# Last stage of a two-layer trunk: raw gate weights in two places and on GpSimd's queue, output weights kept as split parts, and the first split ordered into the stage before

## Chip, cores and metric

The kernel runs on one core of a Trainium2 chip. The metric is the device time of one execution in microseconds. The engines are PE (TensorE), DVE (VectorE), ACT (ScalarE), POOL (GpSimd) and SP (SyncE, which here only issues transfers). PEld is the weight load of TensorE, which runs beside its matmuls.

## What is computed

A sequence of 2048 positions with 1024 features goes through an mLSTM layer, an RG-LRU layer and a last RMSNorm. The change lies in the second half of the RG-LRU layer:

```python
xr, g = jnp.split(proj, [R_WIDTH], axis=-1)          # R_WIDTH = 1536
xc = causal_dwconv(xr, conv_w, conv_b)
xb = xc.reshape(bsz, s, R_BLOCKS, R_BS)               # 8 blocks of 192
r = jax.nn.sigmoid(jnp.einsum('bsnc,ncd->bsnd', xb, w_a).reshape(...) + b_a)
ig = jax.nn.sigmoid(jnp.einsum('bsnc,ncd->bsnd', xb, w_x).reshape(...) + b_x)
log_a = -LRU_C * r * jax.nn.softplus(-lam)
a = jnp.exp(log_a)
bt = jnp.sqrt(-jnp.expm1(2.0 * log_a)) * (ig * xc)
hs = linear_scan(a, bt)
y = hs * jax.nn.silu(g)
return y @ w_out                                      # x + y, then rmsnorm(x, final_g)
```

## The kernel before

Every float32 product is three matmuls (`mm3`, lines 347 to 349): each operand is split into a high part (a cast to a reduced format on ACT, line 720) and a low part (a subtraction on DVE, line 723), and high by high, high by low and low by high are added in PSUM. `split_into` makes the two parts.

The stage before the last, `phase_b1`, ends with a group of the gate projection (`g_out`): four products `pa`, `pb`, `pc`, `pd`, evacuated by ACT or DVE, then a Silu on ACT and a store to `D["g"]` on POOL's queue. Its operands `u11`, `t2`, `t3`, `u21`, `t1`, `t4`, `u22` lie one behind the other at the bottom of on-chip memory, and are last read in the order `u11`, `t2`, `t3`, `u21`, `t1`, `t4`, `u22`. The pools of the next stage take over the same memory, so a tile of the next stage waits for the last reader of the operand it lies on.

The last stage, `phase_b2`, works on four blocks of 512 positions. Each block has 8 gate steps ("g": four groups `p` of three 128-row tiles, two gates each, 7 triples of matmuls to a step) and 24 output steps ("r": 12 row tiles by 2 halves of the output, 4 triples each). The list `steps` interleaves them, one g to three r, with the r of a block 5 g steps behind; so the first five steps of the stage are g steps alone. `weights()` hands out the weights of a step and keeps up to three fetched ahead, at high priority. `fetch` loads a weight and splits it:

- In block 0 a raw gate weight (448 KB) goes through one buffer, `wr`, is split into `wh` and `wl` (two buffers each), and both parts are stored to `D["gw"]` by two transfers on POOL's queue. In later blocks the two parts are loaded from there.
- An output weight (256 KB, three raw buffers) is loaded raw and split in every block.

All weight loads are issued on SP's queue. `load(b, p)` brings the three tiles of a group, `xc`, and splits them; the first of the stage comes by three transfers on ACT's queue. `gates` computes tanh, exp and sqrt on ACT, the products and the scan on DVE, and copies the scan's last column to `hcarry` on POOL. `x2_out` sums a block's output, adds the stored residual `x` (line 1346), and, some steps into the next block, normalizes the eight tiles on DVE (line 1373) and stores them (line 1374) on ACT's queue. The eight buffers of `x2` are reused by the next block.

A planner orders the instructions of each engine and each queue ahead of time, by priorities and modelled costs; every engine and every queue then runs in that order. `order(first, then)` adds an edge that puts `first` ahead of `then` on the same engine.

Of the kernel before, what the change touches and what calls it, by code (L numbers as in the profile page):

```python
# [7 lines left out]
F32 = mybir.dt.float32  # L8
F32R = mybir.dt.float32r
I32 = mybir.dt.int32  # L10
AF = mybir.ActivationFunctionType
# [3 lines left out]
P = 128  # L15
# [3 lines left out]
TB = 512  # L19
# [275 lines left out]
class Trunk:  # L295
# [731 lines left out]
    def phase_b1(self, xT, wout, rwin, D):  # L1027
# [3 lines left out]
        with ExitStack() as ctx:  # L1031
# [116 lines left out]
            def g_out(m2, s):  # L1148
                def out(mi, ni, put):
                    m, n = m2 * 2 + mi, s * 2 + ni  # L1150
                    g = wk("g")[:, 0:TB]
                    put(g)

                    def rest():
                        nc.scalar.activation(g, g, AF.Silu)
                        nc.gpsimd.dma_start(D["g"][m, :, n * TB:(n + 1) * TB], g)
                    return rest
                return out
# [43 lines left out]
    def phase_b2(self, rgate, rwout, D, outT):  # L1202
# [4 lines left out]
        with ExitStack() as ctx:  # L1207
            wp = ctx.enter_context(tc.tile_pool(name="w4", bufs=4, reuse_waits="tile"))
            tp = ctx.enter_context(tc.tile_pool(name="t4", bufs=2, reuse_waits="tile"))
# [11 lines left out]
            def fetch(kind, b, i):  # L1221

                m = 896 if kind == "g" else 512
                wh = wp.tile([P, m], F32R, tag="wh" + kind, name="wh", bufs=2 if kind == "g" else 4)
                wl = wp.tile([P, m], F32R, tag="wl" + kind, name="wl", bufs=2 if kind == "g" else 4)
                if kind == "g" and b > 0:
                    for j, t in enumerate((wh, wl)):
                        nc.sync.dma_start(t.bitcast(F32), D["gw"][i, j])
                    return wh, wl
                raw = wp.tile([P, m], F32, tag="wr" + kind, name="wr", bufs=1 if kind == "g" else 3)  # L1230
                nc.sync.dma_start(raw, rgate[i // 2, :, i % 2 * 896:(i % 2 + 1) * 896] if kind == "g" else
                                  rwout[i % NT, :, i // NT * 512:(i // NT + 1) * 512])
                self.split_into(wh, wl, raw, "a", "v")
                if kind == "g":
                    for j, t in enumerate((wh, wl)):
                        nc.gpsimd.dma_start(D["gw"][i, j], t.bitcast(F32))
                return wh, wl

            def weights():

                with tc.high_priority():
                    while order and len(ready) < 3:
                        ready.append(fetch(*order.pop(0)))
                return ready.pop(0)
# [10 lines left out]
            def load(b, p):  # L1255
# [4 lines left out]
                src = D["xr"][p * 3:p * 3 + 3, :, b * TB:(b + 1) * TB]  # L1260
                if b == 0 and p == 0:
                    for t in range(3):
                        nc.scalar.dma_start(c[:, t], src[t])
                        self.split_into(hi[:, t], lo[:, t], c[:, t], "a", "v")
                else:
                    nc.sync.dma_start(c, src.rearrange("k p t -> p k t"))
                    self.split_into(hi, lo, c, "a", "v")
                return c, hi, lo

            def gates(b, p, xs, ys):  # L1270
# [33 lines left out]
                nc.gpsimd.tensor_copy(hc[:, p * 3:p * 3 + 3], xc[:, :, TB - 1])  # L1304
# [20 lines left out]
            def x2_out(b):  # L1325
# [46 lines left out]
                for m in range(KD):  # L1372
                    nc.vector.scalar_tensor_tensor(x2[m], x2[m], self.v("gf", m), rb, op0=ALU.mult, op1=ALU.mult)
                    (nc.scalar if m % 2 or not last else nc.sync).dma_start(outT[m, :, bs], x2[m])
# [70 lines left out]
def trunk_kernel(tc, xT, woq, wxz, wq, wk, wv, wout, rwin, rgate, rwout, vecs, gbias, outT):  # L1445
    with ExitStack() as ctx:
        K = Trunk(ctx, tc, vecs, gbias)
        D = {}
        for n, shape in (("o", [NTC, P, MI]), ("xm", [16, P, T]), ("xc", [16, P, T]), ("sz", [16, P, T]),
                         ("y", [16, P, T]), ("x1", [KD, P, T]), ("xr", [12, P, T]), ("g", [12, P, T]), ("q", [64, P]), ("dec", [64, P]), ("wx", [16, 4, P, 1024]),  # L1450
                         ("wq", [H, 4, 2, P, 1032]), ("wr", [12, 4, P, 1024]),
                         ("gw", [8, 2, P, 896])):
# [29 lines left out]
```

## Time and profile before

| | us |
|---|---|
| median of 3 runs | 3041.53 |
| lowest and highest | 3035.97, 3041.73 |
| the profiled execution's own time | 3037.02 |
| span of its profile | 3035.2 |
| PE busy | 2916.6 |
| DVE busy | 2126.3 |
| ACT busy | 1503.1 |

Times inside the profile are microseconds from the start of its span. The last product of `phase_b1` starts at 2544.84, and the last stage takes the rest. In a table of windows the busy time of each engine stands with its count of instructions, then the granted TensorE clock as a share of full speed, the mean busy share of the 16 DMA engines, and the rate. In a timeline a row gives the start, the duration, the engine, the line, and in brackets how long the engine idled before it and what ended that. A `q` behind an engine's name is its queue issuing a transfer.

### The profile page before, as it was taken

Reading aid. Unit: us, or ns where it says so; the run is one execution under the profiler, and the core shown is the slowest. Engines: PE = TensorE matmul, PEld = TensorE weight load, DVE = VectorE, ACT = ScalarE, POOL = GpSimd, SP = SyncE. Lnnn points to the kernel's source line nnn. Section 1 sums busy time; section 2 is a strip of 40 time slices with the busy share of each in tenths; the row PEclk is TensorE's granted clock in tenths of the full one; section 3 lists DMA queues with packets and bytes.
Section 4 is the critical chain, followed back from the end, with each engine's and each line's share of the span. In section 5 each row is a group of like instructions: output and inputs, shape, how many; then the busy total and the mean of one; then the engine's idle time right before and its main releaser. Section 6 shows DMA issues by size and latency. Waiting matters only on the chain. (4 is left out here: it accounts for less than half of the span.)

```text
span 3035.2 us, 43861 instructions
## 1 busy us (share of the span) xinstructions
PE 2916.6 (96%) x15730; PEld 2498.7 (82%) x15730; DVE 2126.3 (70%) x3627; ACT 1503.1 (50%) x2512; POOL 431.6 (14%) x786
## 2 busy tenths in 40 slices
PE   7999999999999899999999899999999998899998
PEld 5799987899988898989999677877888886687786
DVE  7766798435465687888888555677778375887775
ACT  6344555324344566666666323233445234876772
POOL 1211132101011111111110111112221111110110
PEclk9999999999999999999999999999999999999999
DMA  6766676767676544444443666566666657756643
GB/s 226 265 222 245 234 253 235 222 192 226 216 227 208 186 142 153 143 155 146 136 146 109 197 191 189 177 203 225 215 212 223 209 184 241 248 181 230 237 135 129
DMA packets 284667, 600.65 MB, mean 198 GB/s; under 512 B 27808, under 2 KB 106400, under 8 KB 284448
## 3 DMA queue, kind: packets, MB, share of 16 engines
q1 hardware_dynamic: 222784, 389.79, 41.4%
q0 software_dynamic: 57200, 199.92, 17.8%
q10 hardware_dynamic: 4464, 8.13, 0.8%
q8 instruction: 124, 2.03, 0.3%
q14 instruction: 95, 0.78, 0.1%
HBM read 388.86 MB, written 208.86 MB: 197 GB/s over the span
## 5 line engine op out<-in xcount | busy, mean ns | idle before, releaser
L720 ACT CAST s<-raw 128x512 fp32r<-128x512 f32 (+1 forms) x360 | 222.3, 621 | 485.2 <-PE acc L349 193.5
L723 DVE TENSOR_TENSOR s<-raw,s 128x512 fp32r<-128x512 f32 (+1 forms) x360 | 246.7, 689 | 68.6 <-ACT s L720 66.4
L347 PE MATMUL acc<-yh,s 128*128 128x512 f32 x512 | 204.0, 400 | 7.3 <-ACT yh L720 3.1
L348 PE MATMUL acc<-yl,s 128*128 128x512 f32 x512 | 203.9, 398 | 1.1 <-DVE yl L723 1.1
L349 PE MATMUL acc<-yh,s 128*128 128x512 f32 x512 | 203.1, 397 | 0.0
L347 PE MATMUL acc<-yh,wh 128*128 128x512 f32 x384 | 150.2, 399 | 16.2 <-ACT yh L720 10.8
L349 PE MATMUL acc<-yh,wl 128*128 128x512 f32 x384 | 150.5, 395 | 1.1 <-DVE wl L723 1.1
L348 PE MATMUL acc<-yl,wh 128*128 128x512 f32 x384 | 151.2, 395 | 0.3 <-DVE yl L723 0.2
L647 DVE SCALAR_TENSOR_TENSOR xc<-xm,vec,xc 128x512 f32<-128x512 f32 x192 | 139.6, 747 | 10.9 <-ACT xc L645 9.1
L720 ACT CAST s<-sum 128x512 fp32r<-128x512 f32 (+1 forms) x120 | 74.0, 617 | 121.9 <-PE pa L349 41.4
L347 PEld LDWEIGHTS acc<-yh,s 128*128 128x128 f32 x512 | 97.1, 190 | 32.9 <-DVE x L1115 3.6
L348 PEld LDWEIGHTS acc<-yl,s 128*128 128x128 f32 x512 | 97.3, 190 | 24.4 <-DVE yl L723 2.2
L349 PEld LDWEIGHTS acc<-yh,s 128*128 128x128 f32 x512 | 97.3, 190 | 22.9
L915 DVE SCALAR_TENSOR_TENSOR C<-C,dl,kv 128x516 f32<-128x516 f32 x112 | 83.7, 747 | 44.6 <-PE kv L349 44.5
L720 ACT CAST wh<-wr 128x512 fp32r<-128x512 f32 (+1 forms) x104 | 65.3, 641 | 97.7 <-PE acc L348 63.1
L647 DVE SCALAR_TENSOR_TENSOR xc<-xr,vec,xc 128x512 f32<-128x512 f32 x144 | 106.1, 747 | 10.0 <-ACT xc L645 8.7
L723 DVE TENSOR_TENSOR wl<-wr,wh 128x512 fp32r<-128x512 f32 (+1 forms) x104 | 73.4, 716 | 51.0 <-ACT wh L720 46.5
L347 PE MATMUL gate<-xch,wh 128*128 128x512 f32 x224 | 91.2, 407 | 18.3 <-ACT wh L720 7.9
L720 ACT CAST Ch<-C 128x516 fp32r<-128x516 f32 x120 | 74.8, 623 | 65.1 <-DVE da L933 47.9
L723 DVE TENSOR_TENSOR s<-sum,s 128x512 fp32r<-128x512 f32 (+1 forms) x120 | 82.5, 688 | 34.1 <-ACT s L720 33.2
L722 DVE CAST yh<-y 128x512 fp32r<-128x512 f32 x63 | 26.9, 426 | 113.2 <-DMA y<-d_y 113.2
L347 PE MATMUL pj<-vwh,xmh 128*128 128x512 f32 x256 | 103.3, 404 | 0.0
(431 smaller groups left out, 9853.4 us busy)
## 6 DMA issues: line engine op xcount, KB each, us to landing
d_wx<-s POOLq DMA_DIRECT2D x64, 512.0 KB, 4.5
s<-d_wx SPq DMA_DIRECT2D x64, 512.0 KB, 4.2
raw<-in_wout_dram SPq DMA_DIRECT2D x128, 256.0 KB, 3.5
raw<-in_wxz_dram SPq DMA_DIRECT2D x124, 256.0 KB, 4.5
d_wr<-s POOLq DMA_DIRECT2D x48, 512.0 KB, 3.3
s<-d_wr SPq DMA_DIRECT2D x48, 512.0 KB, 4.2
wr<-in_rwout_dram SPq DMA_DIRECT2D x96, 256.0 KB, 2.9
raw<-in_rwin_dram SPq DMA_DIRECT2D x84, 256.0 KB, 4.1
```

What stands on the lines that cost most here:

```text
L347: mm(out, sh, mh, start=first, stop=False, skip_group_check=resumed)
L348: mm(out, sh, ml, start=False, stop=False, skip_group_check=resumed)
L349: mm(out, sl, mh, start=False, stop=last, skip_group_check=resumed)
L647: nc.vector.scalar_tensor_tensor(out, x[:, j:j + TB], self.v(wn, m * 4 + j), out, op0=ALU.mult, op1=ALU.add)
L720: a = nc.scalar.copy(hi, src)
L722: a = nc.vector.tensor_copy(hi, src)
L723: b = (nc.gpsimd if lo_eng == "p" else nc.vector).tensor_tensor(lo, src, hi.bitcast(F32), op=ALU.subtract)
L915: nc.vector.scalar_tensor_tensor(C2, C2, self.dl[:, r:r + 1], p2, op0=ALU.mult, op1=ALU.add)
```

## The change

In `phase_b2`:

- The gate weights get a pool of their own, `gp`, allocated first; the pool of the other weights is allocated last.
- Raw weights have two buffers per kind, and in block 0 are loaded on POOL's queue. High and low part now lie in one tile, `both`, two buffers for gates and four for output weights. One transfer stores both parts, and `kept(1)` holds each store back until the next raw load has been issued.
- Output weights are kept too, in the new `D["ow"]`; from block 1 on, both parts (512 KB) are loaded on SP's queue and not split again.
- In block 0 only two gate weights are ready at a time; for the first output weight the priority is raised by 80.
- The split of the first gate weight is ordered ahead of the last four evacuations and Silus of `phase_b1`.
- The first `xc` comes by one transfer on SP's queue.
- The copy of `hcarry` moves from POOL to ACT.
- The output stores of blocks 0 to 2 move from ACT's queue to POOL's, two to an r step.

```diff
@@ g_out
+                    end = s == 1 and m2 == NG - 1
+                    if end and (mi, ni) == (0, 0):
+                        self.tail = []
+                    a = put(g)
+                    if end and (mi, ni) != (0, 0):
+                        self.tail.append(a)
                     def rest():
-                        nc.scalar.activation(g, g, AF.Silu)
+                        a = nc.scalar.activation(g, g, AF.Silu)
+                        if end and (mi, ni) != (0, 0):
+                            self.tail.append(a)
@@ phase_b2
+            gp = ctx.enter_context(tc.tile_pool(name="g4", bufs=2, reuse_waits="tile"))
+            tp = ctx.enter_context(tc.tile_pool(name="t4", bufs=2, reuse_waits="tile"))
             wp = ctx.enter_context(tc.tile_pool(name="w4", bufs=4, reuse_waits="tile"))
-            tp = ctx.enter_context(tc.tile_pool(name="t4", bufs=2, reuse_waits="tile"))
@@ fetch
-                wh = wp.tile([P, m], F32R, tag="wh" + kind, name="wh", bufs=2 if kind == "g" else 4)
-                wl = wp.tile([P, m], F32R, tag="wl" + kind, name="wl", bufs=2 if kind == "g" else 4)
-                if kind == "g" and b > 0:
-                    for j, t in enumerate((wh, wl)):
-                        nc.sync.dma_start(t.bitcast(F32), D["gw"][i, j])
-                    return wh, wl
-                raw = wp.tile([P, m], F32, tag="wr" + kind, name="wr", bufs=1 if kind == "g" else 3)
-                nc.sync.dma_start(raw, rgate[...] if kind == "g" else rwout[...])
-                self.split_into(wh, wl, raw, "a", "v")
-                if kind == "g":
-                    for j, t in enumerate((wh, wl)):
-                        nc.gpsimd.dma_start(D["gw"][i, j], t.bitcast(F32))
-                return wh, wl
+                pool = gp if kind == "g" else wp
+                keep = D["gw" if kind == "g" else "ow"][i]
+                if b > 0:
+                    both = pool.tile([P, 2 * m], F32R, tag="w" + kind, name="w" + kind)
+                    nc.sync.dma_start(both.bitcast(F32), keep)
+                    return both[:, 0:m], both[:, m:2 * m]
+                raw = pool.tile([P, m], F32, tag="wr" + kind, name="wr", bufs=2)
+                nc.gpsimd.dma_start(raw, rgate[...] if kind == "g" else rwout[...])
+                kept(1)
+                both = pool.tile([P, 2 * m], F32R, tag="w" + kind, name="w" + kind)
+                a = self.split_into(both[:, 0:m], both[:, m:2 * m], raw, "a", "v")
+                if kind == "g" and i == 0:
+                    self.order(a, self.tail[-4:])
+                stores.append((keep, both))
+                if i == (7 if kind == "g" else 23):
+                    kept(0)
+                return both[:, 0:m], both[:, m:2 * m]
+            stores = []
+            def kept(n):
+                while len(stores) > n:
+                    keep, both = stores.pop(0)
+                    nc.gpsimd.dma_start(keep, both.bitcast(F32))
@@ weights
-                with tc.high_priority():
-                    while order and len(ready) < 3:
+                while order and len(ready) < 3:
+                    if order[0][0:2] == ("g", 0) and len(ready) == 2:
+                        break
+                    with tc.high_priority(offset=80 if order[0][0:2] == ("r", 0) else None):
                         ready.append(fetch(*order.pop(0)))
@@ load
+                nc.sync.dma_start(c, src.rearrange("k p t -> p k t"))
                 if b == 0 and p == 0:
                     for t in range(3):
-                        nc.scalar.dma_start(c[:, t], src[t])
                         self.split_into(hi[:, t], lo[:, t], c[:, t], "a", "v")
                 else:
-                    nc.sync.dma_start(c, src.rearrange("k p t -> p k t"))
                     self.split_into(hi, lo, c, "a", "v")
@@ gates
-                nc.gpsimd.tensor_copy(hc[:, p * 3:p * 3 + 3], xc[:, :, TB - 1])
+                nc.scalar.copy(hc[:, p * 3:p * 3 + 3], xc[:, :, TB - 1])
@@ x2_out
-                    (nc.scalar if m % 2 or not last else nc.sync).dma_start(outT[m, :, bs], x2[m])
+                    (nc.gpsimd if not last else nc.scalar if m % 2 else nc.sync).dma_start(outT[m, :, bs], x2[m])
+                    if m % 2:
+                        yield
@@ trunk_kernel
-                         ("gw", [8, 2, P, 896])):
+                         ("gw", [8, P, 1792]), ("ow", [24, P, 1024])):
```

## Rows read from the trace of the kernel before

**Rows 1.** Windows, 2500 to 2630: PE, PEld, DVE, ACT, POOL busy, clock, DMA share, GB/s.

```profile
2500.00:2545.00 45.00, 45.00 (x195) 36.26 (x193) 28.21 (x54) 12.00 (x18) 5.94 (x11) 1.00 0.47 151
2545.00:2550.00 5.00, 0.23 (x1) 0.00 (x0) 3.21 (x6) 3.02 (x5) 1.62 (x3) 0.80 0.56 154
2550.00:2580.00 30.00, 22.31 (x71) 15.55 (x72) 9.96 (x10) 19.85 (x25) 3.24 (x6) 0.78 1.02 366
2580.00:2600.00 20.00, 16.87 (x68) 13.06 (x68) 17.47 (x12) 16.59 (x20) 3.85 (x5) 0.95 0.79 277
2600.00:2630.00 30.00, 23.81 (x100) 18.02 (x99) 26.69 (x23) 26.97 (x36) 6.77 (x6) 1.00 0.67 227
```

**Rows 2.** Windows of PE alone: PE busy (matmuls), clock, DMA share, GB/s.

```profile
2545.00:2630.00 85.00, 63.22 (x237) 0.90 0.81 284
2630.00:2735.00 105.00, 102.92 (x458) 1.00 0.60 204
2735.00:2783.00 48.00, 43.62 (x184) 0.96 0.69 235
...
2848.00:2895.00 47.00, 43.20 (x182) 0.96 0.70 239
...
2958.00:3002.00 44.00, 40.13 (x172) 1.00 0.50 167
```

**Rows 3.** The chain that ended last, from the stage's start.

```profile
2550.80 9.92 DMA wr<-in_rgate_dram
2560.75 0.95 ACT wh L720
2561.72 1.10 DVE wl L723
2562.84 6.14 DMA wr<-in_rgate_dram
...
2586.96 4.41 DMA wr<-in_rgate_dram
```

**Rows 4.** Timeline of PE.

```profile
2544.84 0.40 PE L349 MATMUL pd<-u22h,s 128*128 128x512 f32 x1
2551.61 0.80 PE L347 MATMUL gate<-xch,wh 128*128 128x512 f32 x1 [6.38 <-ACT xch L720]
...
2577.56 0.50 PE L347 MATMUL gate<-xch,wh 128*128 128x512 f32 x1 [2.37 <-ACT wh L720]
...
2763.42 2.07 PE L347 MATMUL acc<-yh,wh 128*128 128x512 f32 x4 [4.11 <-ACT yh L720]
```

**Rows 5.** Timelines of SP's and ACT's queues: first raw gate weight, first `xc`.

```profile
2529.27 0.33 SPq L1231 DMA_DIRECT2D wr<-in_rgate_dram  x1
...
2546.01 0.88 ACTq L1263 DMA_DIRECT2D xc<-d_xr  x2
```

**Rows 6.** Timeline of ACT and its queue where block 1 takes over from block 0.

```profile
2738.38 4.69 ACTq L1374 DMA_DIRECT2D out_dram<-x  x5
2743.16 0.62 ACT L720 CAST wh<-wr 128x512 fp32r<-128x512 f32 x1 [4.96 <-DVE x L1373]
2743.39 5.37 ACTq L1374 DMA_DIRECT2D out_dram<-x  x3
2748.80 0.62 ACT L720 CAST wh<-wr 128x512 fp32r<-128x512 f32 x1 [5.02 <-DMA out_dram<-x]
```

**Rows 7.** Transfers by line, 2545 to 2630: count, KB each, median us to landing.

```profile
d_gw<-wl POOLq DMA_DIRECT2D x8, 448.0 KB, 6.5
wr<-in_rgate_dram SPq DMA_DIRECT2D x7, 448.0 KB, 6.1
wr<-in_rwout_dram SPq DMA_DIRECT2D x11, 256.0 KB, 5.0
x<-d_x SPq DMA_DIRECT2D x8, 256.0 KB, 6.9
```

**Rows 8.** Groups on POOL, 2660 to 2960: busy, mean ns, idle before.

```profile
L1304 POOL COPY hcarry<-xc 128x3 f32<-128x3 f32 x11 | 29.0, 2637 | 268.1 <-DVE xc L1302 268.1
```

More of the change, by code (lines that the diff above doesn't have):

```diff
@@ L1151, in out @@
                     g = wk("g")[:, 0:TB]
-                    put(g)
+                    end = s == 1 and m2 == NG - 1
[4 more added lines that the diff above has]
+                        self.tail.append(a)
                     def rest():
-                        nc.scalar.activation(g, g, AF.Silu)
+                        a = nc.scalar.activation(g, g, AF.Silu)
+                        if end and (mi, ni) != (0, 0):
+                            self.tail.append(a)
                         nc.gpsimd.dma_start(D["g"][m, :, n * TB:(n + 1) * TB], g)
@@ L1231, in fetch @@
-                nc.sync.dma_start(raw, rgate[i // 2, :, i % 2 * 896:(i % 2 + 1) * 896] if kind == "g" else
-                                  rwout[i % NT, :, i // NT * 512:(i // NT + 1) * 512])
-                self.split_into(wh, wl, raw, "a", "v")
-                if kind == "g":
-                    for j, t in enumerate((wh, wl)):
-                        nc.gpsimd.dma_start(D["gw"][i, j], t.bitcast(F32))
-                return wh, wl
+                pool = gp if kind == "g" else wp
+                keep = D["gw" if kind == "g" else "ow"][i]
@@ new lines, in fetch @@
+                if b > 0:
[3 more added lines that the diff above has]
+                raw = pool.tile([P, m], F32, tag="wr" + kind, name="wr", bufs=2)
+                nc.gpsimd.dma_start(raw, rgate[i // 2, :, i % 2 * 896:(i % 2 + 1) * 896] if kind == "g" else
+                                    rwout[i % NT, :, i // NT * 512:(i // NT + 1) * 512])
```

## The prediction

> **What bounds the kernel now.** PE is the engine to watch: over the span it is busy 96% of the time, so what a stage can give back is its idle time on PE, and I read that by windows first. Matmuls run at about 0.231 us each when nothing stops them: 195 in 45.00 us just ahead of the stage [rows 1]. The last stage has three kinds of loss [rows 2]. From 2545 to 2630, 237 matmuls need 237 x 0.231 = 54.7 us and take 85: 30 us lost. From 2630 to 2735, 2 us. At the three places where one block takes over from another, PE is idle 4.4, 3.8 and 3.9 us, and at the first two the mean clock is 0.96, worth 1.9 us each: 15.9 us together. The rest of the loss is the end after 3002, which the change leaves alone. So at most about 48 us are to be had.
>
> The chain of waits then says what ends the idle time in the first loss [rows 3]: transfer of a raw gate weight, cast 0.95, subtraction 1.10, next transfer, again and again (9.92, 6.14, down to 4.41 us). With one raw buffer the next transfer can't start before the subtraction ends. In the timeline of PE the first gap is the largest [rows 4]: 6.38 us between the last product before the stage and the first gate product, ended by the cast of `xc`; behind it the mean clock is 0.78 over 30 us [rows 1], because PE had stood still and part of that stretch ran at 1.2 instead of 2.4 GHz. The first `xc` was issued at 2546.01 on ACT's queue, behind ACT's last Silus, while the first raw gate weight had been issued at 2529.27 on SP's [rows 5]. The timeline of ACT at a takeover shows the third loss [rows 6]: ACT stands 4.96 and 5.02 us around its eight output stores, first for DVE's scaled tiles, then for the transfers, and the `yh` that PE waits 4.11 us for is behind it in ACT's order [rows 4].
>
> **The change, part by part.**
>
> *Start of the stage.* The new places of `xc` and of its first parts lie under `t2`, `t3` and `u21`; the last of these is read three products of 12 matmuls before the last group ends, so they are free at about 2545.1 - 3 x 2.77 = 2536.8 [rows 4], and the transfer no longer sits behind ACT's Silus. Two raw gate weights can come before 2545 as well. So the 6.38 us gap should go, and the slow clock behind it with it. The first split, ordered ahead of the last Silus and evacuations, costs ACT 0.95 and DVE 1.10 us there; in the 45 us before the stage ACT is busy 12.00 and DVE 28.21 us [rows 1], so both fit, and nothing on PE waits for those Silus. If the raw weight were late, the last four evacuations and Silus, and behind them their `D["g"]` stores, would wait; these are needed two steps later.
>
> After that three things bound the stretch to 2630, and I work out each.
> - PE alone: 30 us could be saved.
> - ACT: it is busy 3.02 + 19.85 + 16.59 + 26.97 = 66.4 us of these 85 [rows 1]. Two gate casts (0.95 each) and six 512-wide casts (three of `xc`, three of output weights, 0.62 each [rows 6]) can move ahead of 2545: 5.6 us. The remaining 60.8 us at the 0.90 that ACT reached in 2600 to 2630 [rows 1] take 67.6 us: 17 us saved. At full use, 24.
> - DMA: 85 us at 284 GB/s [rows 2] are 24.1 MB. The new stores of output weights add 11 x 0.52 = 5.8 MB by the count of raw loads [rows 7]. Some 3 MB can move ahead of 2545, where the share is 0.47 [rows 1]. The rest, 26.9 MB, takes 73.5 us at the 366 GB/s of the saturated stretch [rows 1]: 11 us saved. Four stores (2.1 MB) and eight residual tiles (2.1 MB) need not be done by then: 22.7 MB, 62 us, 23 saved.
>
> The slots of the split gate weights have a cycle of their own: cast and subtraction 2.05 us, then the store, 6.5 us by the row of `wl` [rows 7] and perhaps 3 more for twice the size, some 11.5 us for two gate steps against 9.7 us of PE. It bounds less tightly than ACT. I take 15 us, between the DMA and the ACT figure, with 8 and 23 as ends.
>
> *On POOL's queue* a raw load has the stores of earlier parts ahead of it and the moved output stores later. Each raw load waits for a split that the store ahead of it waits for too, so the order adds no new wait; transfers issued there landed in 6.5 us against 6.1 for the raw weights on SP's queue [rows 7], which share the stretch. I cost the move between queues at nothing, and at 2 us for each of eight loads if POOL's queue is slower than that row says.
>
> The Trainium skill speaks against expecting bandwidth from it: DMA: Bandwidth & Descriptors, section Issuing engines are not separate DMA queues, says that transfers from the three issuing engines end on the same 16 DMA engines and interleave. The share of 1.02 in 2550 to 2580 agrees, with SP, ACT and POOL all issuing. By that rule only the waiting goes, not the transfer time; a sum that counted all 30 us as gained would be wrong by it.
>
> *Takeovers.* With the output stores off ACT, its two stalls (10 us at each takeover) go, and `ig`, the chain behind it and `yh` come earlier by more than the 4.11 us that PE waits. DVE's eight scalings are spread over four r steps. The 72 casts of output weights in blocks 1 to 3 go (72 x 0.62 = 45 us of ACT), and as many subtractions; most of this lies beside PE and is worth nothing but slack. Against it, each of these steps loads 512 instead of 256 KB on SP's queue: at a takeover 48 us at 235 GB/s are 11.3 MB [rows 2], plus about 11 such loads x 0.26 = 2.9 MB, 14.2 MB in some 43 us, or 330 GB/s, 90% of what was seen at saturation. With four slots a load has some three r steps (3 x 12 x 0.231 = 8.3 us) before PE needs it, where a residual tile in traffic took 6.9 us [rows 7]. So some loads will be late: I take back 1.3 us at each takeover. 15.9 - 3.9 = 12 us gained, with 5 and 16 as ends. In between (0.60 at 204 GB/s [rows 2]) another 60 to 70 GB/s fit.
>
> *`hcarry`* took 2.64 us on POOL, off the path [rows 8]. No row shows it on ACT; it lies between nothing and the 0.62 us of a 512-wide cast. It waits for the scan, with the cast of `yh` behind it, which waits for DVE work behind that scan in any case. Three columns are nearer the low end: I take 0.3 us x 16, hidden under the casts removed, and 0 to 4 us if the cover is gone.
>
> Sum: 3037.0 (the profiled execution) - 15 - 12 = 3010. The median of the runs is 4.5 above that execution; with the same scatter the forecast is 3010 + 3 = **3013 us**, the 3 being a value between the two.
>
> **The rivals.**
> - *Only one of the two parts pays.* If the stretch to 2630 is bound by DMA and the ring of gate slots, or the takeovers by the doubled loads, one of them gives a third of its sum: 15 + 4 or 5 + 12, about 3021 to 3027. For it: the share of 1.02 and the 90% above. Against it: four stores and eight tiles can lag.
> - *POOL's loads are late.* The copy of 128 x 3 elements takes 2.64 us on POOL [rows 8], far longer than its size, while DVE is busy; if DVE delays POOL's issuing likewise, six raw gate loads at about 2.5 us each come late, which takes the 15 us back: 3013 + 15 = 3028. Against it: 6.5 us to landing on that queue. The Trainium skill has this as a rule (SBUF — State Buffer, Who interferes with whom): two-input DVE work keeps GpSimd's reads off a shared port. The long copy agrees; the same section infers that descriptor generation is not held by such DVE work.
> - *Slower: the doubled loads starve PE.* A gate step with its three r steps is 57 x 0.231 = 13.2 us of PE and moves 3 x 0.52 + 0.92 + 0.79 + 0.52 = 3.8 MB in blocks 1 to 3, so 290 GB/s are needed. Takeover windows give 235 / 0.69 = 341 GB/s at full share. If bursts bring the usable rate down to 260, each of 24 steps takes 14.6 us, 1.4 more: +34 - 15 = +19, about 3060. It decides below some 285 GB/s.
> - *No change:* ACT's order at the start turns out as bound as before, and the late loads eat the takeovers: 3036 to 3047.
>
> **How the numbers follow.** The forecast 0.66, one part only 0.15, late POOL loads 0.05, no change 0.06, slower 0.08. This kernel's measurement can tell about 0.2% (6 us) from no change. Faster 0.86, same 0.06, slower 0.08. The forecast's own ends are 3013 - 13 and 3013 + 13; the range goes up to the one-part cases and the late loads: 2999 to 3031.
>
> **What would show it.** Right: the first gate product within 1 us of 2545 and no clock below 1.00 behind it; no idle PE ended by a raw gate weight's cast; the stretch that ended at 2630 ending near 2615; no ACT idle of 5 us at a takeover; PE idle there under 2 us. Wrong: idle PE ended by transfers of `D["ow"]`, or by ACT in the first five steps as long as before; a DMA share of 1.00 through the blocks; POOL's raw loads landing after 8 us or more.

## The result, and the profile after

The changed kernel takes 3049.92 us (median of 9 runs, 3046.71 to 3050.9) against 3038.67 for the kernel before on the same chip: a ratio of 1.0034, 95% interval 1.0025 to 1.0042. It is slower; the forecast was 3013 and faster. The profiled execution after takes 3047.63 us with a span of 3045.9, 10.7 us more than the 3035.2 of before.

Four moments cut both spans: the start of the last product ahead of the stage, and the start of the sums of squares (`ssum`) that close blocks 0, 1 and 2.

| us | start of last product | to block 0's sums | to block 1's | to block 2's | to the end |
|---|---|---|---|---|---|
| before | 2544.8 | 175.3 | 112.5 | 111.9 | 90.7 |
| after | 2545.8 | 184.8 | 112.5 | 108.8 | 94.1 |

The loss is 9.5 us in block 0, where I had forecast 15 of gain. The two takeovers inside the next columns give 0 and 3.1 of gain, and the last column, with the third, costs 3.4; I had forecast 12 of gain for the three together.

The windows of the profile after, all engines (PE, PEld, DVE, ACT, POOL, clock, DMA share, GB/s), for the stretches of [rows 1]:

```profile
2545.00:2550.00 5.00, 1.16 (x5) 0.59 (x4) 2.81 (x4) 2.84 (x5) 2.88 (x6) 0.90 0.61 165
2550.00:2580.00 30.00, 12.27 (x42) 9.58 (x43) 6.73 (x8) 12.06 (x17) 6.24 (x12) 0.62 0.96 364
2580.00:2600.00 20.00, 18.71 (x80) 14.63 (x79) 15.09 (x11) 19.08 (x25) 3.21 (x6) 1.00 0.81 271
2600.00:2630.00 30.00, 26.69 (x105) 20.09 (x104) 27.34 (x22) 28.33 (x35) 5.36 (x10) 0.94 0.75 272
```

In 2550 to 2580 PE does 42 matmuls instead of 71; from 2580 on it does more than before. So one stall ahead of everything costs more than the end of the raw-weight cycle of [rows 3] gives back. The windows of PE alone after, for two of the stretches of [rows 2] (the second 10 us later, as the takeover is):

```profile
2545.00:2640.00 95.00, 65.56 (x253) 0.84 0.83 293
...
2745.00:2793.00 48.00, 44.93 (x191) 0.96 0.86 309
```

The DMA share is up at both, and the takeover does 191 matmuls in 48 us instead of 184. The timeline of PE after, beside [rows 4], has the gaps:

```profile
2545.76 0.40 PE L349 MATMUL pd<-u22h,s 128*128 128x512 f32 x1
2567.72 0.79 PE L347 MATMUL gate<-xch,wg 128*128 128x512 f32 x1 [21.56 <-ACT xch L720]
...
2765.95 0.96 PE L347 MATMUL acc<-yh,wr 128*128 128x512 f32 x3 [2.23 <-ACT yh L720]
...
2878.04 0.50 PE L348 MATMUL acc<-yl,wr 128*128 128x512 f32 x1 [0.83 <-DVE yl L723]
...
2983.49 2.08 PE L347 MATMUL acc<-yh,wr 128*128 128x512 f32 x4 [3.34 <-ACT yh L720]
```

The gap of 6.38 us has become 21.56, with the same releaser, ACT's cast of `xc`. The timeline of ACT says what stands ahead of that cast:

```profile
2546.39 0.92 ACT L720 CAST wg<-wr 128x896 fp32r<-128x896 f32 x1
2547.21 0.63 ACT L1160 ACTIVATE g<-g 128x512 f32<-128x512 f32 x1
2565.43 0.62 ACT L720 CAST wr<-wr 128x512 fp32r<-128x512 f32 x1 [17.59 <-DMA wr<-in_rwout_dram]
2566.53 0.62 ACT L720 CAST wr<-wr 128x512 fp32r<-128x512 f32 x1 [0.48 <-DMA wr<-in_rwout_dram]
2567.05 3.03 ACT L720 CAST xch<-xc 128x512 fp32r<-128x512 f32 x4
```

Two casts of *output* weights, which PE first uses at 2601.8, stand ahead of the casts of `xc`, and the first waits 17.59 us for its transfer. The timeline of SP's queue (beside [rows 5]) gives the issue of `xc`:

```profile
2531.59 3.86 SPq L1282 DMA_DIRECT2D xc<-d_xr  x2
```

The timeline of POOL gives that of the output weight:

```profile
2539.97 1.09 POOL L1239 DMA_DIRECT2D wr<-in_rgate_dram  x2
2546.25 0.54 POOL L1163 DMA_DIRECT2D d_g<-g  x1 [5.19 <-ACT g L1160]
...
2547.38 0.54 POOL L1256 DMA_DIRECT2D d_gw<-wg  x1
...
2549.26 0.54 POOL L1256 DMA_DIRECT2D d_gw<-wg  x1
2549.79 1.07 POOL L1163 DMA_DIRECT2D d_g<-g  x2
2550.85 0.54 POOL L1239 DMA_DIRECT2D wr<-in_rwout_dram  x1
```

`xc` was issued at 2531.59 and landed 5.7 us later, long before 2546. The output weight was issued on POOL at 2550.85, behind gate weights, two stores of pairs (896 KB each) and three stores of `g`, which wait up to 5.19 us for a Silu. The kernel before had its first three output weights on the chip by then, by the timeline of SP's queue:

```profile
2532.06 2.27 SPq L1231 DMA_DIRECT2D wr<-in_rwout_dram  x3
```

These landed after 3.6 us (median), when the DMA engines were less busy (0.47 in 2500 to 2545 [rows 1]). In the changed kernel, the transfers issued in 2545 to 2568 (KB each, median us to landing) went into full DMA engines:

```profile
x<-d_x SPq DMA_DIRECT2D x8, 256.0 KB, 15.7
d_gw<-wg POOLq DMA_DIRECT2D x2, 896.0 KB, 11.6
...
wr<-in_rgate_dram POOLq DMA_DIRECT2D x2, 448.0 KB, 9.3
d_g<-g POOLq DMA_DIRECT2D x3, 256.0 KB, 13.7
wr<-in_rwout_dram POOLq DMA_DIRECT2D x3, 256.0 KB, 12.7
```

In [rows 7] a raw output weight landed in 5.0 us. In the changed kernel, too, the median is 5.7 when the stretch goes to 2630: the first two alone are slow (14.6 and 12.7 us), and they are the ones that count. At a takeover, the timeline of DVE after:

```profile
2748.54 5.38 DVE L1393 SCALAR_TENSOR_TENSOR x<-x,vec,rb 128x512 f32<-128x512 f32 x8
2753.84 1.75 DVE L1318 SCALAR_TENSOR_TENSOR xc<-ig,xc 128x1536 f32<-128x1536 f32 x1
```

And that of ACT (beside [rows 6]):

```profile
2762.64 0.20 ACT L1324 COPY hcarry<-xc 128x3 f32<-128x3 f32 x1 [10.01 <-DVE xc L1322]
...
2764.43 1.47 ACT L720 CAST yh<-g 128x1536 fp32r<-128x1536 f32 x1 [1.00 <-DVE g L1325]
```

The two stalls of ACT are gone, but all eight scalings stand in one lump on DVE ahead of the chain `xc`, `R`, scans, `g` that makes `yh`.

### The profile page after: what moved, and what is told of

The parts are those of the page before. It is cut to its first block, busy times and chain, and to the rows that moved or that the text cites. A ratio compares the mean times of both kernels' runs of the same rounds, so it can differ in the third digit from the quotient of the medians.

```text
span 3045.9 us, 43580 instructions
## 1 busy us (share of the span) xinstructions
PE 2922.9 (96%) x15730; PEld 2502.7 (82%) x15730; DVE 2083.0 (68%) x3555; ACT 1464.2 (48%) x2456; POOL 431.2 (14%) x842
## 5 line engine op out<-in xcount | busy, mean ns | idle before, releaser
L347 PE MATMUL acc<-yh,wr 128*128 128x512 f32 x384 | 151.8, 403 | 10.5 <-ACT yh L720 10.3
L348 PE MATMUL acc<-yl,wr 128*128 128x512 f32 x384 | 156.1, 407 | 3.6 <-DVE yl L723 3.6
L349 PE MATMUL acc<-yh,wr 128*128 128x512 f32 x384 | 155.0, 404 | 0.0
L347 PE MATMUL gate<-xch,wg 128*128 128x512 f32 x224 | 88.8, 400 | 22.4 <-ACT xch L720 21.8
L349 PE MATMUL pj<-vwh,xml 128*128 128x512 f32 x256 | 100.3, 392 | 0.0
L348 PE MATMUL pj<-vwl,xmh 128*128 128x512 f32 x256 | 100.0, 391 | 0.0
```

Source lines behind the costliest of these rows:

```text
L347: mm(out, sh, mh, start=first, stop=False, skip_group_check=resumed)
L348: mm(out, sh, ml, start=False, stop=False, skip_group_check=resumed)
L349: mm(out, sl, mh, start=False, stop=last, skip_group_check=resumed)
```

## The experiments

The table gives each profile's four columns as above; the times are medians of all executions, and the ratios, with their 95% interval, are against the kernel before on the same chip. The runs are from several chips, so runs of different chips are compared by ratio or by column. In kernels whose engines do block 0 in the same order, its column still differs by up to 1.1 (before, e7, e14, e17), 2.1 (e9, e11, e16) and 3.9 us (after, e4); a difference that small in one profile shows nothing.

| kernel | us | ratio (95%) | block 0 | 1 | 2 | end |
|---|---|---|---|---|---|---|
| e1 first `xc` ahead of output weights | 3047.45 | 1.0025 (1.0015 to 1.0035) | 186.4 | 111.4 | 108.8 | 92.7 |
| e5 raw output weights on SP | 3033.41 | 0.9979 (0.9969 to 0.9988) | 172.5 | 114.4 | 108.8 | 91.0 |
| e9 = e5 + residuals held | 3034.89 | 0.9978 (0.9969 to 0.9988) | 170.8 | 112.7 | 108.8 | 92.9 |
| e15 = e11 + three places | 3040.02 | 0.9994 (0.9986 to 1.0003) | 182.9 | 109.0 | 109.0 | 90.9 |
| e4 stores on ACT again | 3052.53 | 1.0041 (1.0026 to 1.0056) | 188.7 | 111.9 | 108.5 | 95.8 |
| e7 before + stores on POOL | 3033.56 | 0.9972 (0.9963 to 0.9981) | 176.4 | 109.9 | 109.9 | 89.8 |
| e11 = e9 + scalings behind chain | 3028.77 | 0.9959 (0.9945 to 0.9972) | 171.5 | 109.0 | 109.1 | 92.2 |
| e16 = e11 once more | 3030.69 | 0.9967 (0.9954 to 0.9979) | 169.4 | 109.0 | 109.0 | 92.1 |
| e17 = e7 + scalings behind chain | 3027.45 | 0.9964 (0.9950 to 0.9977) | 176.3 | 107.8 | 107.8 | 87.7 |
| e3 `hcarry` on POOL | 3053.2 | 1.0044 (1.0029 to 1.0059) | 192.3 | 111.9 | 108.8 | 90.7 |
| e21 = e11, `hcarry` on POOL | 3043.16 | 1.0005 (0.9991 to 1.0019) | 183.4 | 109.1 | 109.1 | 91.5 |
| e8 output weights not kept | 3064.02 | 1.0081 (1.0066 to 1.0096) | 189.0 | 115.0 | 115.7 | 92.6 |
| e19 = e11, not kept | 3031.45 | 0.9971 (0.9959 to 0.9983) | 166.0 | 110.7 | 117.0 | 88.5 |
| e20 = e19, `hcarry` on POOL | 3045.26 | 1.0013 (1.0004 to 1.0023) | 179.6 | 110.5 | 116.4 | 89.2 |

### What makes the stall at the start

**e1** orders only the casts of the first `xc` ahead of the first three output weights' casts.

```diff
+                if kind == "r" and i < 3:
+                    self.order(self.x0, a)
-                        self.split_into(hi[:, t], lo[:, t], c[:, t], "a", "v")
+                        self.x0 += self.split_into(hi[:, t], lo[:, t], c[:, t], "a", "v")
```

> The changed kernel with one more edge in ACT's and DVE's order: the split of the first xc ahead of the splits of the first three output weights. Theory T (order): in the changed kernel the first gate product came at 2567.7 because the cast of xc stood in ACT's order behind two casts of output weights, whose raw transfers landed at 2565. Then the first gate product comes at 2546 to 2549 here. But the two casts still stand ahead of ACT's first tanh, so PE can run only two gate steps, up to 8 PSUM banks, and ACT waits for the same transfer: I expect 5 to 10 us less than the changed kernel, 3040 to 3045. Rival R (traffic): the DMA engines were saturated from 2550 to 2568, so xc and the gate weights would not be there either; then the first gate product stays after 2560 and the time within 3 us of the changed kernel's 3050.

The first gate product starts at 2549.03 after a gap of 2.42, as the theory said, but the 5 to 10 us did not come: the kernel is no faster beyond its scatter. The timeline of ACT in e1:

```profile
2548.37 1.64 ACT L720 CAST xch<-xc 128x512 fp32r<-128x512 f32 x3
2566.82 0.62 ACT L720 CAST wr<-wr 128x512 fp32r<-128x512 f32 x1 [16.81 <-DMA wr<-in_rwout_dram]
```

The stall has moved behind that cast, and PE stands 13.01 us behind the first two gate steps, for a gate weight's cast behind the same output weight. The order of one cast isn't the cause; an ACT that waits in order for a late transfer is.

**e5** issues the raw output weights of block 0 on SP, as before, and leaves everything else of the change.

```diff
-                nc.gpsimd.dma_start(raw, rgate[...] if kind == "g" else rwout[...])
+                (nc.gpsimd if kind == "g" else nc.sync).dma_start(raw, rgate[...] if kind == "g" else rwout[...])
```

> The changed kernel with the raw output weights of block 0 issued on SP's queue again; the raw gate weights stay on POOL's. The planner then puts the casts of xc ahead of those of output weights. Theory T: no engine waits long at the start, the first gate product comes before 2549, the sum of block 0 (ssum) some 15 us earlier than in the changed kernel, and the time is 3030 to 3037. Rival R (traffic): the first product is early, but the next weights come late because the same bytes go over saturated DMA engines; ssum of block 0 gains less than 7 us, time 3043 to 3048.

Faster than before: this one line takes 12.3 us off block 0. The timeline of ACT in e5:

```profile
2550.29 3.02 ACT L720 CAST xch<-xc 128x512 fp32r<-128x512 f32 x4
...
2572.80 0.94 ACT L720 CAST wg<-wr 128x896 fp32r<-128x896 f32 x1 [2.10 <-DMA d_gw<-wg]
...
2574.23 0.61 ACT L720 CAST wr<-wr 128x512 fp32r<-128x512 f32 x1
```

The output weight's cast now comes 24 us after those of `xc` and waits for nothing. The DMA engines are as full as after (share 1.01 and 1.03 in the first two tens of us from 2550). Two things changed at once. The first two of these loads are issued 0.14 and 1.13 us behind the last product, where they were 5.09 and 8.09 on POOL, and they land after 5.7 and 14.6 us: 5.8 and 15.8 us behind the last product instead of 19.6 and 20.7. And their casts stand behind those of `xc`. Had both casts stayed ahead, ACT would have come to `xc` some 16.4 us behind the last product instead of 21.3; so by my estimate about 5 us of PE's shorter wait are the transfers' and the rest is the order's. No run has one without the other. The Trainium skill says in DMA: Bandwidth & Descriptors, section Issuing engines are not separate DMA queues, that transfers of all issuing engines interleave on the same 16 engines; this trace agrees: SP's second load took 14.6 us beside stores on POOL's queue that took 13.8 (median).

**e9** adds to e5 that the loads of block 0's eight residual tiles (2 MB) wait behind the load of the next block's first `xc`.

```diff
+                if (b, p) == (1, 0):
+                    self.held = (d,)
+                        if b == 0:
+                            self.order(self.held, (d,))
```

> The changed kernel with the raw output weights of block 0 on SP's queue, as in the run that had only that, and the eight loads of block 0's second half of x1 (2 MB) held behind the load of the next block's first xc. If what is left of the start's loss (idle PE of 2.3, 3.7, 1.7, 2.4 and 4.2 us) is the full DMA engines, 2 MB less at some 410 GB/s are 5 us: 3026 to 3031 us, and the transfers of 2545 to 2570 land in 8 us and less. Rival (ACT and DVE pace the first products): 3032 to 3036 us, the gaps as they were.

The rival holds by the median, 3034.89, and by the gaps: 2.19, 3.31, 1.62 and 2.41 us, as in e5. The times alone would not decide, since four of the ten executions took 3029.01 to 3031.10. The windows of 2580 to 2590 (columns as above) show why, first in e5:

```profile
2580.00:2590.00 10.00, 6.71 (x15) 4.47 (x15) 10.00 (x8) 9.12 (x14) 1.60 (x3) 0.50 1.01 396
```

And in e9:

```profile
2580.00:2590.00 10.00, 6.86 (x17) 4.72 (x17) 10.00 (x8) 9.27 (x13) 1.41 (x3) 0.53 0.84 287
```

The DMA share fell from 1.01 to 0.84 and PE hardly went faster: DVE is busy all the time there and ACT nearly. The granted clock is 0.50 and 0.53 there, the lower level, and what it adds isn't separated. In 2550 to 2570 the engines stayed full in e9 too (share 1.01; the medians to landing are 7.3 to 19.0 us, where I had expected 8 and less), so for the gap near 2576 the traffic isn't ruled out: in e5 a cast of ACT ahead of it waits 2.10 us for the store of a gate pair.

**e15** gives gate pairs three places (and `xc` three instead of four) on top of e11 (below).

```diff
-                c = tp.tile([P, 3, TB], F32, tag="xc", name="xc", bufs=4)
+                c = tp.tile([P, 3, TB], F32, tag="xc", name="xc", bufs=3)
-                both = pool.tile([P, 2 * m], F32R, tag="w" + kind, name="w" + kind)
+                both = pool.tile([P, 2 * m], F32R, tag="w" + kind, name="w" + kind, bufs=3 if kind == "g" else 4)
```

> The fastest kernel so far (raw output weights on SP's queue, residuals held, scalings spread), with three places for a gate weight's pair of parts instead of two, and three for xc instead of four to make room. ACT there stands 1.9 us at 2570 for the store of an earlier pair, with the next xc's cast behind it. Theory (that place is what is left of the start's stall of 3.3 to 3.9 us near 2576): the stall goes and 2 to 4 us come off, 3025 to 3027 us. Rival (ACT, busy 8 to 9.3 of 10 us in 2570 to 2590, paces these products, or xc is late with three places): 3028 to 3032 us.

A miss of both theories: the wait near 2576 did go, but block 0 is 13.5 us longer than in e16. The timeline of ACT:

```profile
2558.11 0.94 ACT L720 CAST wg<-wr 128x896 fp32r<-128x896 f32 x1 [7.34 <-DMA wr<-in_rgate_dram]
2558.95 3.03 ACT L720 CAST xch<-xc 128x512 fp32r<-128x512 f32 x4
```

With a third place free, the third gate weight's cast moved ahead of the casts of `xc`, and the same kind of stall came back: PE stands 10.96 us, 8.9 more than the 2.07 of e16. What makes the rest of the 13.5 is open, and the place taken from `xc` may have a part in it. A free place can lengthen a path, when it lets a later cast be put earlier in an engine's order.

### What the takeovers hold

**e4** puts the stores of blocks 0 to 2 back on ACT and drops the hand-over after each second scaling.

```diff
-                    (nc.gpsimd if not last else nc.scalar if m % 2 else nc.sync).dma_start(outT[m, :, bs], x2[m])
-                    if m % 2:
-                        yield
+                    (nc.scalar if m % 2 or not last else nc.sync).dma_start(outT[m, :, bs], x2[m])
```

> The changed kernel, with the output stores of blocks 0 to 2 issued from ACT again and without the extra hand-over after each second scaling. Theory (the start of the stage loses some 10 us, the takeovers between blocks give back almost nothing because DVE's eight scalings stand in one lump ahead of the chain to yh): issuing the stores from ACT puts ACT's two stalls of some 5 us back at each takeover, in which nothing ends later than DVE's lump, so 3048 to 3056 us, and the idle PE at the takeovers 3 to 6 us each. Rival (the stores on GpSimd's queue are worth the 4 us each that I forecast): 3058 to 3064 us. Rival (the stores' place costs something): under 3046 us.

3052.53, within the first theory's range; blocks 1 and 2 are not longer than after, so in the changed kernel the stores' move was worth nothing there. The idle PE of 3 to 6 us at each takeover didn't come: it is 2.79 and 0.55 at the first two. At the third PE stands 7.60 us, and the end is 1.7 longer. The timeline of PE in e4 has the releaser:

```profile
2994.00 0.77 PE L347 MATMUL acc<-yh,wr 128*128 128x512 f32 x1 [7.60 <-DMA wr<-d_ow]
```

That is the load of a kept pair. By the timeline of ACT the cast of `yh` ends at 2993.54, only 0.5 us before, so without the load most of the wait would still have been there.

**e7** makes only that move, in the kernel before (the same line, without the hand-over).

> The kernel before, with nothing changed but the queue of the output stores of blocks 0 to 2, now GpSimd's. My forecast for this part was 12 us: 3027 us. Theory now (ACT's stall only gives way to DVE's lump of scalings and the longer chain behind it): 3031 to 3040 us, with PE still idle 3 to 5 us at each takeover. Rival (the part gains by itself and is spoilt by something else of the change): 3024 to 3029 us.

3033.56: the move gives 2.6 and 2.0 us at two takeovers and 0.9 at the end, 5.4 by the profile and 7.7 by the medians. The timeline of DVE in e7 shows what is late next:

```profile
2739.84 5.38 DVE L1373 SCALAR_TENSOR_TENSOR x<-x,vec,rb 128x512 f32<-128x512 f32 x8
2745.14 1.75 DVE L1298 SCALAR_TENSOR_TENSOR xc<-ig,xc 128x1536 f32<-128x1536 f32 x1
```

The lump was there before too, hidden behind ACT's stall. PE still waits 1.85 us.

**e11** adds to e9 that scalings 2 to 7 of blocks 0 to 2 follow the chain on DVE.

```diff
-                nc.vector.tensor_tensor(g, xc, g, op=ALU.mult)
+                self.chain = (nc.vector.tensor_tensor(g, xc, g, op=ALU.mult),)
-                    nc.vector.scalar_tensor_tensor(x2[m], x2[m], self.v("gf", m), rb, op0=ALU.mult, op1=ALU.mult)
+                    a = nc.vector.scalar_tensor_tensor(x2[m], x2[m], self.v("gf", m), rb, op0=ALU.mult, op1=ALU.mult)
+                    if m >= 2 and not last:
+                        self.order(self.chain, (a,))
```

> As the run with the held residuals, and scalings 2 to 7 of blocks 0 to 2 ordered behind the chain (xc, R, three scans, g) on DVE. If the lump of eight scalings (5.4 us) on DVE is what now sets yh, the chain starts some 4 us sooner at each takeover and the idle PE there (3.1, 0.8 and 3.3 us) goes: 5 to 8 us below the run with the held residuals. Rival (yh is set elsewhere, or the scalings behind the chain stop DVE's next work and come back later): within 2 us of it.

6.1 us below e9 by the medians, as expected, and 4.1 by the three later columns: block 1 is 3.7 shorter, and PE's wait at the first takeover falls from 2.55 + 0.82 to 1.32.

**e14** meant to do the same in e7.

> The kernel before with two things: the output stores of blocks 0 to 2 on GpSimd's queue, and scalings 2 to 7 of these blocks ordered behind the chain xc, R, scans, g on DVE. With the stores alone the chain starts at 2745.1, when the lump of eight scalings (5.4 us) ends, while ig is there at about 2743; PE is idle 1.8 us at each takeover. Theory (after the stores, the lump is what is late next): chain some 2 us sooner, PE's idle time at the takeovers under 0.5 us, 3028 to 3031 us. Rival (ACT's casts of output weights, which this kernel still has, or the scalings behind the chain are as late): 3032 to 3036 us.

The edit had no effect: without the hand-overs all eight scalings are written out ahead of the chain that they should follow, so DVE's order is that of e7. It is a second measurement of e7: 3035.26 (ratio 0.9983, 0.9975 to 0.9992) beside 3033.56, with columns of 175.4, 109.9, 109.9 and 89.8.

**e17** does it with the hand-overs.

> The kernel before with the output stores of blocks 0 to 2 on GpSimd's queue, a hand-over after each second scaling, and scalings 2 to 7 behind the chain on DVE. In the run before this one the order had no effect, because all eight scalings were written out ahead of the chain that they should follow; now they do follow it. Theory (behind the stores the lump of eight scalings is what is late next): the chain starts some 2 us sooner than with the stores alone, PE is idle under 0.5 us at each takeover instead of 1.8, 3029 to 3032 us. Rival (ACT's casts of output weights in this kernel, or the scalings behind the chain, are as late): 3033 to 3037 us.

3027.45, better than expected, though PE's wait of 0.99 is longer than the 0.5 expected. The timeline of DVE in e17:

```profile
2742.34 1.41 DVE L1373 SCALAR_TENSOR_TENSOR x<-x,vec,rb 128x512 f32<-128x512 f32 x2
2745.58 1.76 DVE L1298 SCALAR_TENSOR_TENSOR xc<-ig,xc 128x1536 f32<-128x1536 f32 x1 [1.83 <-ACT ig L1291]
```

Two scalings stand ahead of the chain, and the chain waits for `ig` instead of them. Two edits at the takeovers of the kernel before, with nothing of the rest of the change, give as much as the mended whole (ratio 0.9964 against 0.9959 and 0.9967). **e16** is e11 once more, on the chip of e14 and e15.

> The fastest version so far once more, on the same chip as the two beside it: 3026 to 3031 us. If the kernel before with its two edits at the takeovers comes within 2 us of it, then two places for raw gate weights, the earlier first split and the kept output weights are worth no more together than those two edits at the takeovers.

### The parts costed at nothing, and the rival

**e3** puts only `hcarry` back on POOL in the changed kernel; **e21** does it in e11.

```diff
-                nc.scalar.copy(hc[:, p * 3:p * 3 + 3], xc[:, :, TB - 1])
+                nc.gpsimd.tensor_copy(hc[:, p * 3:p * 3 + 3], xc[:, :, TB - 1])
```

> The changed kernel with the copy of hcarry back on POOL. In the changed kernel ACT stood 8 to 10 us at this copy at each takeover, waiting for DVE's scan. Theory H: this wait holds up yh, so without it PE's waits at the takeovers (2.2, 0.8, 3.3 us) go and the time falls by 3 to 8 us. Rival D: the wait only mirrors DVE, where the eight scalings of the outputs stand in one piece of 5.4 us ahead of the chain that leads to yh; then ACT waits for the same DVE work at yh and the time stays within 2 us of the changed kernel.

> The fastest kernel with the change's start, output weights kept, with only hcarry moved back to GpSimd. Theory A: 3027 to 3032 us, as with hcarry on ACT. Theory B: blocks 1 and 2 and the end 5 to 7 us shorter, 3022 to 3026 us.

In e3 PE's wait at the first takeover is 0.7 us shorter and the others are the same, while block 0 is 7.5 us longer. e21 fell outside both theories by its median: blocks 1 and 2 are as in e16, but block 0 is 14.0 us longer. Not every execution lost that: one of its ten took 3028.10. The timeline of POOL in e21:

```profile
2579.03 0.55 POOL L1239 DMA_DIRECT2D wr<-in_rgate_dram  x1 [2.13 <-DVE wg L723]
2582.42 7.17 POOL L1326 COPY hcarry<-xc 128x3 f32<-128x3 f32 x1 [2.84 <-issue]
2589.55 0.54 POOL L1256 DMA_DIRECT2D d_gw<-wg  x1
...
2628.33 0.19 POOL L1326 COPY hcarry<-xc 128x3 f32<-128x3 f32 x1 [2.78 <-DVE xc L1324]
```

In e16 that store is issued at 2578.81, 10.7 us sooner. The first copy lasts 7.17 us, until DVE's work, unbroken since 2572.71, ends at 2589.54; the one at 2628.33, where DVE stands still for 0.35 us, lasts 0.19, and on ACT it takes 0.20. The copy holds SP's queue too, since the next `xc` comes into the place that it reads. From the waits of SP's queue in e21:

```profile
SPq L1282 <- POOL hcarry L1326: 4.0, 1, 4.0
```

e16 has no such wait. Raw output weights are issued behind that `xc`; ACT waits 6.70 us for one at 2609.42, and PE 6.90 behind it. How much of the 14.0 us comes by either queue isn't separated. The rule of the Trainium skill that I weighed before (SBUF — State Buffer, Who interferes with whom), that two-input DVE work keeps GpSimd off a shared port, agrees, and so does its inference on descriptors: POOL's issues take 0.53 to 0.55 us each, with DVE busy too.

**e8** drops the keeping of output weights in the changed kernel (blocks 1 to 3 load them raw on SP and split them); **e19** does so in e11, and **e20** puts `hcarry` on POOL besides.

```diff
-                if b > 0:
+                if b > 0 and kind == "g":
-                stores.append((keep, both))
+                if kind == "g":
+                    stores.append((keep, both))
```

> The changed kernel without keeping the output weights: loaded raw (256 KB) and split in every block as before the change, on POOL's queue in block 0 and on SP's later; no stores of them. Theory L: the doubled loads in blocks 1 to 3 and the stores in block 0 cost; without them the time falls by 3 us or more. Rival K: the 72 splits that keeping removes were worth more than the bytes cost; the time rises by 3 us or more. In between: both small, within 3 us of the changed kernel's 3050.

> The fastest kernel with the change's start (raw output weights on SP's queue, residuals held, scalings spread), but its output weights not kept: each block loads them raw and splits them again. It separates the price of the doubled loads in blocks 1 to 3. Theory A (the kept pairs cost there what they save: idle PE ended by their loads, 2.0 us, and loads that take up the DMA engines): blocks 1 and 2 take 107.8 us each and the end 88 to 90, as in the kernel before with the stores and scalings moved, so 3021 to 3026 us. Theory B (hcarry on ACT, in order ahead of yh, costs it): the casts added to ACT stand behind hcarry too, and it is slower than the kernel that keeps, 3032 to 3040 us.

> As the run before, and hcarry on GpSimd as in the kernel before. Theory A: no different from the run before, 3021 to 3026 us. Theory B: this one, and not the run before, takes 107.8 us for blocks 1 and 2: 3021 to 3026 us, 8 us and more below it.

e8 is 14.1 us above the changed kernel, with 5.42, 5.77 and 4.56 us of idle PE at the takeovers. In e19 neither theory holds as a whole: block 0 is 3.4 shorter than in e16 (it has no stores of output weights) and the end 3.6, blocks 1 and 2 are 1.7 and 8.0 longer. Keeping is worth 2.6 us by these profiles and hardly more than the scatter by the medians (3031.45 beside 3028.77 and 3030.69). e20, outside both theories as well, is 13.6 us slower than e19 in block 0, the second sight of `hcarry`'s cost; SP's queue waits 4.0 us for a copy there too.

## Why the prediction was wrong

**The raw-weight cycle.** Right: no idle PE after is ended by a gate weight's cast, and the cycle of [rows 3] is gone.

**"So the 6.38 us gap should go."** This step failed, and with it the sign. `xc` came as early as I said, and the raw gate weights were issued at 2539.97. But I read "free early" as "used early". What decides most is ACT's order, and I did not ask where the output weights' casts, whose priority the change also touches, would stand in it. They came out ahead of `xc`'s casts. The gap of 21.56 us takes 15.2 more than before, of which block 0 gets 5.7 back. My ACT term also counted three casts of output weights as work that can move ahead of 2545. In every kernel with the change these loads are issued behind the last product, 0.14 us at the earliest (e5), where the kernel before issued them 12.8 us ahead of it; whether the new place in memory or the planner keeps them there isn't shown.

The gain that the rest of the start was good for is seen in e5, and with residuals held in e9, e11 and e16: 2.8 to 5.9 us, against my 15. In 2580 to 2590 ACT and DVE pace the products, at the lower clock. I had bounds for PE, ACT and DMA and none for DVE, which is busy 10.00 of 10 us there.

**"The order adds no new wait."** Wrong, on POOL's queue. Each raw gate load does wait for splits that its store waits for too. The output weights don't: their first loads need no split, yet they stood behind stores of gate pairs and of `g`. The late raw weight that I had named did come about: ACT's first split waits 5.40 us for it, and POOL's store of `g` 5.19 for the Silu behind. That is so in e5 as well (5.42 and 5.20), which is fast, so it doesn't decide. My price for a slow queue was 2 us for each load, laid on PE directly; in fact one load, 14.6 us to landing, stopped ACT for 17.59 us. The medians of [rows 7] over 85 us hid what the saturated first 20 us do. The rival *POOL's loads are late* had the right queue and the wrong reason: POOL's issues took 0.53 to 0.55 us beside a busy DVE, and it was the output weights, not the gate weights, that came late. *No change* named ACT's order at the start, but only as bound as before; it was worse.

**The takeovers, 12 us.** ACT's stalls went, as predicted, but "spread over four r steps" did not happen: the lump of 5.38 us became what is late next. The stores' move alone is worth 5 to 8 us (e7), the lump 4 to 6 (e11 against e9; e17 against e7, by column and by median), so 12 is about what both together give (e17: 11.5 by the medians). That the size fits is chance: it is that of two edits, and the change had made one. In the changed kernel even that one shows nothing in blocks 1 and 2 (e4).

**Doubled loads, and the rival that they starve PE.** No idle PE after is ended by a kept pair's load; the 1.3 us that I took back at each takeover were not seen there. The DMA share in 2745 to 2793 is 0.86, where I had 90% of saturation. Such waits do appear in other kernels: the longest is 0.6 to 2.0 us in e11, e15, e16 and e21, and one ends the 7.60 us of e4. That of e16 lies behind the third takeover:

```profile
2980.04 0.50 PE L347 MATMUL acc<-yh,wr 128*128 128x512 f32 x1 [1.98 <-DMA wr<-d_ow]
```

**`hcarry`, "hidden".** Its time on ACT, 0.20 us, was right. That it "waits for the scan, with `yh` behind it" cost nothing is borne out by e21's blocks 1 and 2. What I missed is the other side: with POOL now issuing the weights' loads and stores, the copy there costs 14.0 and 13.6 us in block 0 (e21, e20); the 7.5 of e3 is less sure, since kernels of one order differ by up to 3.9. I priced the move by where the work went and not by what it uncovered.

**Slips in the sums.** Two, and neither moves the forecast: one part alone gives 3021 to 3023, not 3027, and 16 copies at 0.3 us are 4.8 us, not 4.

**Open.** In e17, blocks 1 and 2 are 1.2 us shorter each than in e16 and the end 4.4; keeping accounts for most of the end (e19) and I have no cause for the rest. The end of kernels that keep output weights lies between 90.7 and 95.8, so I don't assign the 3.4 us there. The start of e16 with the later blocks of e17 would give 472.7 us by the sum of columns, against 479.5 for e16; it wasn't run.

## What to carry to other kernels

Ask of a buffer or a queue that is freed not only what can start sooner, but what the in-order engines will then put first: one operation that waits for a late transfer stops all behind it, and with full DMA engines a 256 KB load took 12.7 to 14.6 us to landing behind others in its queue, where the last one took 5. When a stall on one engine is removed, look at the same stretch of the next engine in the chain before taking the whole wait as gain; here the next one was some 2 us behind (PE's wait went from 4.11 to 1.85 in e7). Price the start of a stage from the first transfers in it, not from a median over the stage.

## What the hardware showed that I had not expected

- A copy of 128 x 3 elements on GpSimd lasted as long as DVE's row of work beside it: 7.17 us at one place, 2.64 in the mean of [rows 8], against 0.19 where DVE stood still (e21) and 0.20 on ACT.
- The granted clock of TensorE fell after a gap of only 2.19 us. The timeline of PE in e9:

```profile
2548.53 0.40 PE L349 MATMUL pd<-u22h,s 128*128 128x512 f32 x1
2551.12 0.50 PE L347 MATMUL gate<-xch,wg 128*128 128x512 f32 x1 [2.19 <-ACT xch L720]
...
2553.29 0.63 PE L348 MATMUL gate<-xcl,wg 128*128 128x512 f32 x1
2553.72 0.63 PE L349 MATMUL gate<-xch,wg 128*128 128x512 f32 x1
...
2555.54 0.40 PE L348 MATMUL gate<-xcl,wg 128*128 128x512 f32 x1
2555.78 0.39 PE L349 MATMUL gate<-xch,wg 128*128 128x512 f32 x1
```

PE had run without a stop, and the granted clock is 1.00 in 2540 to 2548, the level of 2.4 GHz. After the gap it is 0.50 in 2553 to 2555, 1.2 GHz, with products 0.43 us apart, and 0.98 in 2555 to 2560, with products 0.23 us apart. Closing most of a gap did not save the slow stretch behind it.
- With the DMA engines full (394 to 413 GB/s in 2550 to 2570), the landing of a residual tile on SP's queue went from 6.9 us [rows 7] to 15.7, and that of a raw output weight from 5.0 to 12.7 on POOL's (medians). On SP's, the two of e5 took 5.7 and 14.6 us.
